# Row-alternated attention products in the second layer, and division after the value products in the third

## Chip, cores and metric

The kernel runs on one core of one Trainium2 chip. The metric is device time in microseconds (us) of one execution, as a median over runs. TensorE is called PE here, its weight loads PEld, VectorE DVE, ScalarE ACT, GpSimd POOL, and SyncE, which issues most transfers, SP.

## The reference

One forward pass over 256 tokens of width 1024 through three layers. The first (latent attention, an RWKV recurrence and 32 experts) is untouched by the change. The second has two attention mixers, the third has one with three branches; both end in a gated feed-forward network. Cut to what the change touches:

```python
# second layer, mixer A ("dsa"): index scores choose keys, then latent attention
rel = relu(einsum('bqhd,bsd->bqhs', iq, ik) * IDX_DIM ** -0.5)       # 8 heads of 64
score = einsum('bqhs,bqh->bqs', rel, iw)                            # causal, top_k(score, 64)
q_lat = einsum('bthd,hdc->bthc', q_nope, w_uk)                      # 8 heads, 64 -> 128
s = einsum('bqhc,bqkc->bqhk', concat[q_lat, q_rope], kg) * A_SCALE  # 128 + 32 deep
o = softmax(s) @ c_kv                                               # then w_uv
# second layer, mixer B ("diff"): two softmaxes m = 0, 1 per head, 4 heads
s = einsum('bqhmd,bshmd->bhmqs', q, k) * B_QK_DIM ** -0.5           # 64 deep
a = softmax(s)[:, :, 0] - lam_full * softmax(s)[:, :, 1]
o = einsum('bhqs,bshe->bqhe', a, v)
# third layer ("nsa"): 16 heads in 4 groups; compressed, selected and window branches
out = g[..., 0:1] * o_cmp + g[..., 1:2] * o_slc + g[..., 2:3] * o_win
```

## The kernel before, in words

Everything lies with tokens or features on the 128 partitions, in two token halves j = 0, 1; half 1 sees 256 keys (nk = 256), half 0 sees 128. Large weights stream from HBM and are split by ACT (`whi`, L304) and DVE or POOL (`wlo`, L308, L306) into two fp32r parts, so that a product is three cheap matmuls (L297 to L299). These run all the time and are called **fill** here: whenever a mixer waits for another engine, PE does fill. Up to six split weight tiles are kept ready ahead of PE.

The mixers' own products are plain fp32. One such product is two records in the trace, since PE makes two passes over each weight load pair. Many of them are only 64 or 32 deep, so that they use rows 0 to 63 or 64 to 127 of PE (or a strip of 32), and leave the other rows free. PSUM has 8 banks; `bank(K)` takes one, of 512 fp32 columns per partition.

**Second layer.** Four generators are interleaved by `weave`: the fill stream, `dsa_index`, `diff` and `dsa`. A generator yields a cost and a lag in us, by which `weave` decides who writes its instructions next; a scheduler then fixes each engine's order, within which every engine works strictly in turn. `pipe` runs a list of units through stages, one unit later per stage.

- `dsa_index`: for each half (1 first) four visits to PE. A visit takes one parity `par` of heads, thus one row half, and does two matmuls (L2063) into one bank; then ReLU on ACT and weighted sums on DVE, later eight rounds of maximum and replacement on DVE.
- `diff`: six units (half, first head, heads, m). Products of a unit (L2235, rows chosen by m) each followed by the causal mask, added by a bf16 matmul with an identity (L2237). Then DVE maximum (L2239), ACT exponentials with sums, division (L2262 combines m = 0 and 1), transposes on PE (L2271), products with the values (L2287).
- `dsa` starts when fill and `diff` are through: `qlT` by eight matmuls of 64 rows (L2105), copied by ACT and DVE (L2110). Then eight units (j, h0) of two heads; per head a 128-deep latent product (L2130), a 32-deep rope product in strip h0 (L2131) and the mask (L2132), all into one bank. Then maximum (L2134), exponentials (L2139), reciprocal and multiply (L2148), and transposes on PE (L2158).

**Third layer.** Here the order is as written. `pace` puts fill between the steps of `nsa`, which sends 28 units through scores, weigh, turn, values and out. 24 are ordinary (one or two heads, two branches s) and 4 are compressed (one per group). `weigh` takes the reciprocal, multiplies by the gate, and scales the 512 columns of exponentials on DVE (L2622); `turn` transposes (L2633), copies; `values` (L2657, L2645) accumulates all units of a group in one long-lived bank, which ACT copies when a half is complete (L2561); `out` transposes.

Of the kernel before, what the change touches and what calls it, by code (L numbers as in the profile page):

```python
# [2011 lines left out]
def dsa_index(K, pool, T, S, D, done):  # L2012
# [42 lines left out]
    for j in (1, 0):  # L2055
# [36 lines left out]
def dsa(K, pool, T, S, D, mix, done):  # L2092
# [8 lines left out]
    for b in range(0, 4, 2):  # L2101
        for par in range(2):
            p = bank(K)
            for bb in range(2):
                nc.tensor.matmul(p[:, bb * 256:bb * 256 + 256], wuk[rows[par], b + bb, :], T["qnT"][rows[par], b + bb, :],  # L2105
                                 start=True, stop=True)
# [6 lines left out]
            yield 0.9  # L2113
# [5 lines left out]
    prs = {}  # L2119

    def scores(u):
        j, h0 = u
        nk = 128 * (j + 1)
        js = slice(j * 128, j * 128 + 128)
        r = slice(h0 * 32, h0 * 32 + 32)
        p = bank(K)
        for i in range(2):
            h = h0 + 4 * i
            o = p[:, i * nk:i * nk + nk]
            nc.tensor.matmul(o, qlT[h % 2][:, h // 2, js], ckvT[:, :nk], start=i == 0, stop=False, skip_group_check=True)  # L2130
            nc.tensor.matmul(o, T["qrT"][r, i, js], krT[r, :nk], start=False, stop=False, skip_group_check=True)  # L2131
            nc.tensor.matmul(o, K.identb, mk[j], start=False, stop=True, skip_group_check=True)  # L2132
# [8 lines left out]
        return 0.98 * (j + 1)  # L2141
# [62 lines left out]
def diff(K, pool, T, S, mix, done):  # L2204
# [21 lines left out]
    prs, aTs, pos = {}, {}, {}  # L2226

    def scores(u):
        j, h0, hp, m = u
        nk = 128 * (j + 1)  # L2230
        js = slice(j * 128, j * 128 + 128)
        p = bank(K)
        for i in range(hp):
            oo = p[:, i * nk:(i + 1) * nk]
            nc.tensor.matmul(oo, qb[rows[m], h0 + i, js], kb[rows[m], h0 + i, :nk], start=i == 0, stop=False,  # L2235
                             skip_group_check=True)
            nc.tensor.matmul(oo[:, js], K.identb, K.causb, start=False, stop=True, skip_group_check=True)  # L2237
# [9 lines left out]
        return 1.1  # L2247
# [265 lines left out]
def nsa(K, pool, T, mix, done):  # L2513
# [34 lines left out]
    pos, mixed = {}, []  # L2548

    def into(u):  # L2550

        new = u.b not in pos
        if new:
            pos[u.b] = bank(K)
        return pos[u.b], new

    def ends(u):
        u.O = {}
        for j in u.ends:
            u.O[j] = pool.tile([128, 256], F32, name="Onsa", bufs=2)  # L2560
            nc.scalar.activation(u.O[j], pos[u.b][:, j * 256:j * 256 + 256], AF.Copy)  # L2561

    def scores(u):
        b = u.b
        if u.j is None:

            pc = bank(K)
            u.pr = s3 = pool.tile([128, 2, 2, 2, 16], F32, name="s3", bufs=2)
# [36 lines left out]
    def weigh(u):  # L2605
# [12 lines left out]
        for ii in range(u.hp):  # L2618
            h = 4 * u.b + 2 * (u.i0 + ii) + u.par
            for s in range(2):  # L2620
                q = (ii * 2 + s) * u.nk
                nc.vector.tensor_scalar(u.pr[:, q:q + u.nk], u.pr[:, q:q + u.nk], den[:, u.j, h, s:s + 1], None, op0=OP.mult)  # L2622

    def turn(u):
        pt = bank(K)
        if u.j is None:
            for j in range(2):
                nc.tensor.transpose(pt[LOP, j * 128:j * 128 + 128], u.pr[:, j].rearrange("p i s n -> p (i s n)"), K.ident)
            u.pT = pool.tile([64, 256], F32, name="pcT", bufs=2)
# [11 lines left out]
    def values(u):  # L2641
        if u.j is None:
            po, new = into(u)
            for j in range(2):
                nc.tensor.matmul(po[:, j * 256:j * 256 + 256], u.pT[:, j * 128:j * 128 + 128],  # L2645
                                 T["vbd"][:, u.b].rearrange("p h d -> p (h d)"), start=new and j == 0, stop=bool(u.ends),
                                 skip_group_check=True)
            ends(u)
            return 0.9
        j, g = u.j, u.b  # L2650
        po, new = into(u)
        for ii in range(u.hp):
            o = j * 256 + (2 * (u.i0 + ii) + u.par) * 64
            for s in range(2):
                for b in range(j + 1):
                    bb = (ii * 2 + s) * (j + 1) + b
                    nc.tensor.matmul(po[:, o:o + 64], u.pT[:, bb * 128:bb * 128 + 128], vsw[:, b, s, g * 64:g * 64 + 64],  # L2657
                                     start=new and ii + s + b == 0, stop=s == 1 and b == j, skip_group_check=True)
        ends(u)
        return 0.9  # L2660

    def out(u):
        for j in u.ends:
            p = bank(K)
            for k in range(2):
                nc.tensor.transpose(p[:, k * 128:k * 128 + 128], u.O[j][:, k * 128:k * 128 + 128], K.ident)
# [228 lines left out]
```

## Time and profile before

| what | value |
|---|---|
| median of 3 runs (lowest, highest) | 1305.43 us (1299.16, 1306.05) |
| the profiled execution, own time | 1300.7 us |
| its span, first to last instruction | 1298.9 us |
| PE busy | 1236.4 us, 95% |
| DVE busy | 905.1 us, 70% |
| ACT busy | 746.3 us, 57% |
| POOL busy | 161.8 us, 12% |
| mean granted PE clock | 0.979 of full speed |

Times inside the span count from its start. The second layer's mixers stand at about 570 to 712 us, the third's at about 960 to 1090 us. A matmul's start is a record; its end is modelled and overlaps the next one's start, so prices here go from start to start. The granted clock has two levels, 1.0 (2.4 GHz) and 0.5 (1.2 GHz); a mean between them tells the share of each.

### The profile page before, as it was taken

What the parts mean: (1) busy time and instruction counts of PE and PEld (TensorE: products, weight loads), DVE (VectorE), ACT (ScalarE), POOL (GpSimd) and SP (SyncE); (2) the same over time, 40 slices, a digit from 0 to 9 for tenths busy, and PEclk for the clock granted to TensorE, in tenths of its full rate; (3) what the DMA queues carried; (4) which work ended last, traced back from release to release, by engine and by line L of the source; (5) the groups of instructions that cost most, each with busy time, mean ns of one, the idle gap of its engine ahead of it and who ended that gap; (6) DMA issues with size and microseconds to landing.
All of it is one profiled execution on the core that took longest, in us unless ns stands there. A gap on an engine that the chain in (4) does not pass through costs nothing.

```text
span 1298.9 us, 21081 instructions
## 1 busy us (share of the span) xinstructions
PE 1236.4 (95%) x7798; PEld 1072.3 (83%) x7798; DVE 905.1 (70%) x1779; ACT 746.3 (57%) x1540; POOL 161.8 (12%) x245
## 2 busy tenths in 40 slices
PE   7898999999989999999999999999899998999997
PEld 7687998778868888788866899988878877999986
DVE  5688546889989999867966555564567776655462
ACT  6864314779879898764453444454355554544451
POOL 7134002000010000011110000000057321000000
PEclk9899989889989999999999999999999999999999
DMA  9322007788979999564312365575242313655560
GB/s 282 112 98 82 1 2 241 256 291 334 344 268 336 338 382 321 167 189 143 113 50 65 114 196 172 186 249 173 89 129 85 111 33 98 202 173 172 184 227 33
DMA packets 124282, 228.71 MB, mean 176 GB/s; under 512 B 10720, under 2 KB 86832, under 8 KB 124176
## 3 DMA queue, kind: packets, MB, share of 16 engines
q1 hardware_dynamic: 122672, 223.83, 50.5%
q0 software_dynamic: 1504, 3.49, 1.0%
q8 instruction: 63, 1.03, 0.3%
q14 instruction: 43, 0.35, 0.1%
HBM read 226.25 MB, written 1.05 MB: 175 GB/s over the span
## 4 chain that ended last, share of the span: by engine, by line
PE 48%; DVE 4%; ACT 2%; issue 1%; DMA 1%; POOL 0%; DVEq 0%; POOLq 0%; ACTq 0%
PE ps L297 13%; PE ps L299 13%; PE ps L298 13%; PE ps L2657 1%; DMA raw<-in_ev_w_in_dram 1%; DVE pr L2622 1%; DVE wlo L308 1%; PE ps L1918 1%; PE ps L2633 1%; PE ps L2235 1%; PE ps L2131 1%; PE ps L2592 1%; PE ps L2475 1%; PE ps L2063 1%; ACT whi L304 0%
## 5 line engine op out<-in xcount | busy, mean ns | idle before, releaser
L308 DVE TENSOR_TENSOR wlo<-raw,whi 128x512 fp32r<-128x512 f32 (+1 forms) x797 | 510.9, 690 | 79.4 <-ACT whi L304 77.2
L304 ACT ACTIVATE whi<-raw 128x512 fp32r<-128x512 f32 (+1 forms) x821 | 476.9, 625 | 123.1 <-PE ps L299 38.3
L297 PE MATMUL ps<-hTh,whi 128*128 128x256 f32 (+1 forms) x1032 | 301.3, 292 | 1.2 <-ACT whi L304 1.2
L299 PE MATMUL ps<-hTh,wlo 128*128 128x256 f32 (+1 forms) x1032 | 292.2, 283 | 0.2 <-DVE wlo L308 0.2
L298 PE MATMUL ps<-hTl,whi 128*128 128x256 f32 (+1 forms) x1032 | 291.8, 283 | 0.0
L297 PEld LDWEIGHTS ps<-hTh,whi 128*128 128x128 f32 (+1 forms) x1032 | 196.5, 190 | 6.0 <-issue 3.2
L298 PEld LDWEIGHTS ps<-hTl,whi 128*128 128x128 f32 (+1 forms) x1032 | 197.3, 191 | 2.7 <-issue 2.4
L299 PEld LDWEIGHTS ps<-hTh,wlo 128*128 128x128 f32 (+1 forms) x1032 | 196.0, 190 | 0.4 <-DVE wlo L308 0.4
L297 PE MATMUL ps<-whi,xh 128*128 128x512 f32 x256 | 104.2, 407 | 0.0
L298 PE MATMUL ps<-wlo,xh 128*128 128x512 f32 x256 | 101.8, 397 | 0.0
L299 PE MATMUL ps<-whi,xl 128*128 128x512 f32 x256 | 101.5, 397 | 0.0
L272 POOL TENSOR_TENSOR nrs<-nv,mhalf 128x1 f32<-128x1 f32 x10 | 5.6, 556 | 629.6 <-DVE nv L1716 629.6
L304 ACT ACTIVATE hh<-sl 128x512 fp32r<-128x512 f32 x20 | 12.6, 632 | 115.0 <-DVE sl L1808 115.0
L1808 DVE TENSOR_TENSOR sl<-sl,ps 128x512 f32<-128x512 f32 x20 | 13.8, 688 | 88.8 <-PE ps L299 88.8
L298 PE MATMUL ps<-wlo,hh 128*128 128x512 f32 x176 | 69.6, 395 | 0.0
L297 PE MATMUL ps<-whi,hh 128*128 128x512 f32 x176 | 69.3, 394 | 0.0
L297 PE MATMUL ps<-whi,hTh 128*128 128x256 f32 (+3 forms) x192 | 61.0, 319 | 6.3 <-ACT hTh L304 4.4
L299 PE MATMUL ps<-whi,hTl 128*128 128x256 f32 (+3 forms) x192 | 60.4, 316 | 1.3 <-DVE hTl L308 1.3
L298 PE MATMUL ps<-wlo,hTh 128*128 128x256 f32 (+3 forms) x192 | 60.0, 313 | 0.8 <-DVE wlo L308 0.8
L299 PEld LDWEIGHTS ps<-whi,xl 128*128 128x128 f32 x256 | 48.5, 189 | 11.1
L297 PEld LDWEIGHTS ps<-whi,xh 128*128 128x128 f32 x256 | 48.6, 190 | 10.1
L298 PEld LDWEIGHTS ps<-wlo,xh 128*128 128x128 f32 x256 | 48.7, 190 | 9.9
(878 smaller groups left out, 2218.5 us busy)
## 6 DMA issues: line engine op xcount, KB each, us to landing
raw<-in_w_gate_dram SPq DMA_DIRECT2D x64, 512.0 KB, 5.2
raw<-in_w_up_dram SPq DMA_DIRECT2D x64, 512.0 KB, 6.1
raw<-in_w_down_dram SPq DMA_DIRECT2D x32, 1024.0 KB, 6.8
raw<-in_ffn_w_gate_dram SPq DMA_DIRECT2D x22, 1024.0 KB, 5.4
raw<-in_ffn_w_up_dram SPq DMA_DIRECT2D x22, 1024.0 KB, 5.9
raw<-in_ffn_w_down_dram SPq DMA_DIRECT2D x22, 1024.0 KB, 5.1
raw<-in_ev_w_in_dram SPq DMA_DIRECT2D x11, 1024.0 KB, 5.7
raw<-in_od_w_in_dram SPq DMA_DIRECT2D x10, 1024.0 KB, 5.2
```

What stands on the lines that cost most here:

```text
L297: nc.tensor.matmul(ps, lh, rh, start=start, stop=False, **kw)
L298: nc.tensor.matmul(ps, lh, rl, start=False, stop=False, **kw)
L299: nc.tensor.matmul(ps, ll, rh, start=False, stop=stop, **kw)
L304: K.nc.scalar.activation(hi, src, AF.Copy)
L308: K.nc.vector.tensor_tensor(lo, src, hi.bitcast(F32), op=OP.subtract)
L1808: nc.vector.tensor_tensor(sl, sl, pu, op=OP.mult)
L1918: nc.tensor.matmul(p2, c[f"R{d}"], z.rearrange("p b t -> p (b t)"), start=True, stop=True)
L2063: nc.tensor.matmul(p[:, bb * nk:bb * nk + nk], T["iqT"][rows[par], b0 + bb, j * 128:j * 128 + 128], ikT[rows[par], :nk], start=True, stop= ...
L2131: nc.tensor.matmul(o, T["qrT"][r, i, js], krT[r, :nk], start=False, stop=False, skip_group_check=True)
L2235: nc.tensor.matmul(oo, qb[rows[m], h0 + i, js], kb[rows[m], h0 + i, :nk], start=i == 0, stop=False, skip_group_check=True)
L2475: nc.tensor.matmul(p[:, :60], w1[:, i, :], tmp[:, i].rearrange("p g n -> p (g n)"), start=i == 0, stop=i == 15)
L2592: nc.tensor.matmul(o, q2[r], KL[r, b, :, :u.nk], start=False, stop=False, skip_group_check=True)
```

## The change

In the second layer, products that use different rows of PE are issued alternately into two banks: index visits take both parities at once, `diff` takes m = 0 and 1 in one visit, `dsa` takes the units h0 and h0 + 1 in one visit, with rope products of two strips alternating and masks last. The yielded costs follow. In the third layer, exponentials are transposed undivided; each unit's values go to a bank of its own, and DVE divides, gates and adds the 64 columns of each head and branch from PSUM into an SBUF sum. The compressed units' scores and their transposes move to the common ring of 8 tiles (`w2k`).

```diff
             for par in range(2):
-                p = bank(K)
-                for bb in range(2):
-                    nc.tensor.matmul(p[:, bb * nk:bb * nk + nk], T["iqT"][rows[par], b0 + bb, j * 128:j * 128 + 128],
-                                     ikT[rows[par], :nk], start=True, stop=True)
+            ps = [bank(K), bank(K)]
+            for bb in range(2):
+                for par in range(2):
+                    nc.tensor.matmul(ps[par][:, bb * nk:bb * nk + nk], T["iqT"][rows[par], b0 + bb, j * 128:j * 128 + 128],
+                                     ikT[rows[par], :nk], start=True, stop=True)
...
-                yield 0.43 * (j + 1), 0.8
+                yield 0.25 * (j + 1), 0.8
...
+    def products(j, hs):
+        nk = 128 * (j + 1)
+        js = slice(j * 128, j * 128 + 128)
+        for h0 in hs:
+            sps[j, h0] = bank(K)
+        o = lambda h0, i: sps[j, h0][:, i * nk:i * nk + nk]
+        for h0 in hs:
+            for i in range(2):
+                h = h0 + 4 * i
+                nc.tensor.matmul(o(h0, i), qlT[h % 2][:, h // 2, js], ckvT[:, :nk], start=i == 0, stop=False, skip_group_check=True)
+        for i in range(2):
+            for h0 in hs:
+                r = slice(h0 * 32, h0 * 32 + 32)
+                nc.tensor.matmul(o(h0, i), T["qrT"][r, i, js], krT[r, :nk], start=False, stop=False, skip_group_check=True)
+        for h0 in hs:
+            for i in range(2):
+                nc.tensor.matmul(o(h0, i), K.identb, mk[j], start=False, stop=True, skip_group_check=True)
...
-        return 0.98 * (j + 1)
+        return 1.5 * (j + 1) if h0 % 2 == 0 else 0.0
...
+    def products(j, h0, hp):
+        nk = 128 * (j + 1)
+        js = slice(j * 128, j * 128 + 128)
+        ps = [bank(K), bank(K)]
+        for i in range(hp):
+            for m in range(2):
+                nc.tensor.matmul(ps[m][:, i * nk:(i + 1) * nk], qb[rows[m], h0 + i, js], kb[rows[m], h0 + i, :nk], start=i == 0,
+                                 stop=False, skip_group_check=True)
+        for m in range(2):
+            for i in range(hp):
+                nc.tensor.matmul(ps[m][:, i * nk:(i + 1) * nk][:, js], K.identb, K.causb, start=False, stop=True,
+                                 skip_group_check=True)
+            sps[j, h0, hp, m] = ps[m]
...
-        for ii in range(u.hp):
-            h = 4 * u.b + 2 * (u.i0 + ii) + u.par
-            for s in range(2):
-                q = (ii * 2 + s) * u.nk
-                nc.vector.tensor_scalar(u.pr[:, q:q + u.nk], u.pr[:, q:q + u.nk], den[:, u.j, h, s:s + 1], None, op0=OP.mult)
...
+        for ii in range(u.hp):
+            i = 2 * (u.i0 + ii) + u.par
+            oh = O[:, i * 64:i * 64 + 64]
+            for s in range(2):
+                o = po[:, (ii * 2 + s) * 64:(ii * 2 + s) * 64 + 64]
+                d = den[:, j, 4 * g + i, s:s + 1]
+                if (g, j, i) in begun:
+                    nc.vector.scalar_tensor_tensor(oh, o, d, oh, op0=OP.mult, op1=OP.add)
+                else:
+                    nc.vector.tensor_scalar(oh, o, d, None, op0=OP.mult)
+                begun.add((g, j, i))
```

The order of the instructions at three places. First PE at the start of `dsa`, where `qlT` is made (buffer numbers shown; ps_7731, ps_7735 and so on are banks). Before:

```order
L1918 MATMUL ps_7724<-rz_7721,cst_b_6659 128x512
L2105 MATMUL ps_7731<-qnT_7438,wuk2_2343 128x256 x2
L2105 MATMUL ps_7735<-qnT_7438,wuk2_2343 128x256 x2
L2105 MATMUL ps_7739<-qnT_7438,wuk2_2343 128x256 x2
L2105 MATMUL ps_7743<-qnT_7438,wuk2_2343 128x256 x2
L2130 MATMUL ps_7751<-ckvT_6892,qlT0_7729 128x256
```

Now:

```order
L1918 MATMUL ps_7724<-rz_7721,cst_b_6659 128x512
L2108 MATMUL ps_7731<-qnT_7443,wuk2_2343 128x256
L2108 MATMUL ps_7732<-qnT_7443,wuk2_2343 128x256
L2108 MATMUL ps_7731<-qnT_7443,wuk2_2343 128x256
L2108 MATMUL ps_7732<-qnT_7443,wuk2_2343 128x256
L2108 MATMUL ps_7739<-qnT_7443,wuk2_2343 128x256
L2108 MATMUL ps_7740<-qnT_7443,wuk2_2343 128x256
L2108 MATMUL ps_7739<-qnT_7443,wuk2_2343 128x256
L2108 MATMUL ps_7740<-qnT_7443,wuk2_2343 128x256
```

The eight matmuls are the same and back to back in both; two of one row half in a row became one of each in turn.

Second, PE a little later, up to the first transposes of `dsa` (pr2_7760 and pr2_7767 are the first unit's exponentials). Before, the second unit and six transposes of `diff`'s output stand ahead of them:

```order
L2130 MATMUL ps_7767<-ckvT_6892,qlT1_7730 128x256
L2131 MATMUL ps_7767<-krT_6893,qrT_7720 128x256
L2132 LDWEIGHTS identb_370
L2132 MATMUL ps_7767<-selm_7311,identb_370 128x256
L2308 MATMUL ps_7779<-cst_i_90,odf_7423 128x128 x2
L2308 MATMUL ps_7784<-cst_i_90,odf_7423 128x128 x2
L2308 MATMUL ps_7789<-cst_i_90,odf_7423 128x128 x2
L2158 MATMUL ps_7795<-cst_i_90,pr2_7760 128x128 x4
```

Now:

```order
L2141 MATMUL ps_7751<-krT_6893,qrT_7720 128x256
L2141 MATMUL ps_7752<-krT_6893,qrT_7720 128x256
L2141 MATMUL ps_7751<-krT_6893,qrT_7720 128x256
L2141 MATMUL ps_7752<-krT_6893,qrT_7720 128x256
L2144 LDWEIGHTS identb_370
L2144 MATMUL ps_7751<-selm_7311,identb_370 128x256
L2144 LDWEIGHTS identb_370
L2144 MATMUL ps_7751<-selm_7311,identb_370 128x256
L2144 LDWEIGHTS identb_370
L2144 MATMUL ps_7752<-selm_7311,identb_370 128x256
L2144 LDWEIGHTS identb_370
L2144 MATMUL ps_7752<-selm_7311,identb_370 128x256
L2177 MATMUL ps_7780<-cst_i_90,pr2_7767 128x128 x4
```

The products of units 0 and 1 come together, and the transposes of unit 0 follow the last mask with nothing between; the transposes of `diff`'s output (L2308, now L2338) come only after units 2 and 3.

Third, DVE in one step of the third layer, as one piece of the difference (`Onsa` is the new sum):

```order
-L2616 RECIPROCAL den_10402<-den_10402 128x2
-L2617 TENSOR_TENSOR den_10402<-den_10402,gts 128x2
-L2622 TENSOR_SCALAR pr_10882<-pr_10882,den_10402 128x256 x2
-L2638 COPY pT_10960<-ps 128x512
-L2595 TENSOR_REDUCE mx_10401<-ps 128x2x2
+L2639 RECIPROCAL den_10402<-den_10402 128x2
+L2640 TENSOR_TENSOR den_10402<-den_10402,gts 128x2
+L2656 COPY pT_10955<-ps 128x512
+L2618 TENSOR_REDUCE mx_10401<-ps 128x2x2
+L2697 TENSOR_SCALAR Onsa<-ps,den_10402 128x64
+L2695 SCALAR_TENSOR_TENSOR Onsa<-ps,den_10402,Onsa 128x64
 L1921 TENSOR_TENSOR qf<-ps,qf 128x512
```

The two multiplies of 256 columns ahead of the copy and the maximum are gone; two operations of 64 columns from PSUM stand behind them. On PE the order of the third layer's products is what it was.

## Rows read from the trace of the kernel before

**Rows 1.** Windows: us, busy time and instructions of PE, PEld, DVE, ACT, POOL, clock, DMA, GB/s.
```profile
560.00:600.00 40.00, 37.70 (x290) 36.36 (x289) 26.04 (x47) 21.81 (x45) 6.70 (x18) 0.94 0.64 198
600.00:640.00 40.00, 40.00 (x265) 33.42 (x264) 34.50 (x87) 15.99 (x30) 0.00 (x0) 1.00 0.39 132
...
1050.00:1080.00 30.00, 25.97 (x139) 19.31 (x139) 23.95 (x53) 14.56 (x49) 12.49 (x12) 0.94 0.16 52
1080.00:1100.00 20.00, 20.00 (x101) 16.72 (x100) 13.21 (x27) 8.40 (x20) 0.57 (x1) 0.91 0.42 135
```
**Rows 2.** Waits of PE from 940 to 1110 us: total, times, longest.
```profile
PE ps L2633 <- DVE pr L2622: 7.7, 10, 1.5
```
**Rows 3.** Timeline of PE in the first layer: start, busy, line, operands, count.
```profile
114.49 1.16 PE L960 MATMUL ps<-bt,AR 64*128 64x128 f32 x16
...
127.26 1.13 PE L990 MATMUL ps<-AR,kt 64*128 64x256 f32 x8
```
**Rows 4.** Timeline of PE, index visits of half 1 and of half 0.
```profile
602.88 0.28 PE L298 MATMUL ps<-hTl,whi 128*128 128x256 f32 x1
603.00 0.28 PE L299 MATMUL ps<-hTh,wlo 128*128 128x256 f32 x1
603.21 1.13 PE L2063 MATMUL ps<-ikT,iqT 64*128 64x256 f32 x4
...
604.50 0.28 PE L298 MATMUL ps<-hTl,whi 128*128 128x256 f32 x1
...
626.58 0.71 PE L2063 MATMUL ps<-ikT,iqT 64*128 64x128 f32 x4
```
**Rows 5.** Timeline of PE in `diff`, a unit of half 1 and one of half 0.
```profile
636.49 0.70 PE L2235 MATMUL ps<-kbT,qbT 64*128 64x256 f32 x2
...
638.15 0.28 PE L298 MATMUL ps<-hTl,whi 128*128 128x256 f32 x1
...
654.30 0.48 PE L2235 MATMUL ps<-kbT,qbT 64*128 64x128 f32 x2
...
656.68 0.28 PE L298 MATMUL ps<-hTl,whi 128*128 128x256 f32 x1
```
**Rows 6.** Timeline of PE in `dsa`: `qlT`, a head of half 1, a head of half 0.
```profile
665.82 2.10 PE L2105 MATMUL ps<-qnT,wuk 64*128 64x256 f32 x16
...
669.22 0.60 PE L2130 MATMUL ps<-ckvT,qlT 128*128 128x256 f32 x2
669.75 0.69 PE L2131 MATMUL ps<-krT,qrT 32*128 32x256 f32 x2
...
670.50 0.60 PE L2130 MATMUL ps<-ckvT,qlT 128*128 128x256 f32 x2
...
685.53 0.39 PE L2130 MATMUL ps<-ckvT,qlT 128*128 128x128 f32 x2
...
686.33 0.44 PE L2130 MATMUL ps<-ckvT,qlT 128*128 128x128 f32 x2
```
**Rows 7.** Timeline of DVE at the start of `dsa`.
```profile
669.17 1.28 DVE L2110 COPY qlT<-ps 128x512 f32<-128x512 f32 x2
670.70 0.69 DVE L2134 TENSOR_REDUCE mx<-ps 128x2 f32<-128x512 f32 x1 [0.24 <-PE ps L2132]
...
673.85 0.68 DVE L2148 TENSOR_TENSOR pr<-pr,den 128x512 f32<-128x512 f32 x1
```
**Rows 8.** Timeline of PE, first transposes of `dsa`.
```profile
674.68 0.63 PE L2158 MATMUL ps<-cst_i,pr 128*128 128x128 f32 x4 [0.82 <-ACT mxh L2309]
```
**Rows 9.** Groups by line from 940 to 1110 us: busy, mean ns, idle before.
```profile
L2622 DVE TENSOR_SCALAR pr<-pr,den 128x256 f32<-128x256 f32 (+1 forms) x64 | 30.8, 536 | 1.2
```
**Rows 10.** Line L2622 on DVE: shortest, median and longest in ns.
```profile
L2622 DVE TENSOR_SCALAR pr<-pr,den x64: 272/349/1370, 970.1 to 1081.2; 128x256 f32<-128x256 f32 x32, 128x128 f32<-128x128 f32 x32
```
**Rows 11.** Timeline of DVE: a small copy from PSUM; one late unit's multiplies.
```profile
962.99 0.25 DVE L2366 COPY gts<-ps 128x96 f32<-128x96 f32 x1
...
1075.81 3.92 DVE L2622 TENSOR_SCALAR pr<-pr,den 128x128 f32<-128x128 f32 x4
```

More of the change, by code (lines that the diff above doesn't have):

```diff
@@ L2101, in dsa @@
     for b in range(0, 4, 2):
+        ps = [bank(K), bank(K)]
+        for bb in range(2):
+            for par in range(2):
+                nc.tensor.matmul(ps[par][:, bb * 256:bb * 256 + 256], wuk[rows[par], b + bb, :], T["qnT"][rows[par], b + bb, :],
+                                 start=True, stop=True)
         for par in range(2):
[L2103 to L2106, printed above, removed]
+            p = ps[par]
             dst = qlT[par][:, b:b + 2, :]
@@ L2123, in scores @@
         nk = 128 * (j + 1)
[L2124 to L2132, printed above, removed]
+        if h0 % 2 == 0:
+            products(j, (h0, h0 + 1))
+        p = sps.pop(u)
         mv = mx[:, j, h0:8:4]
@@ L2230, in scores @@
         nk = 128 * (j + 1)
[L2231 to L2237, printed above, removed]
+        if m == 0:
+            products(j, h0, hp)
+        p = sps.pop(u)
         mv = mx[:, j, m, h0:h0 + hp]
@@ L2246, in scores @@
                                  accum_out=den[:, j, m, h:h + 1])
-        return 1.1
+        return 0.0 if m else 1.4
     def weigh(u):
@@ L2547, in nsa, with into @@
             [u for u in g if u.j == 1][-1].ends = (1,)
[L2548 to L2561, printed above, removed]
+    sums, begun, mixed = {}, set(), []
+    def into(b, j):
+        if (b, j) not in sums:
+            sums[b, j] = pool.tile([128, 256], F32, name="Onsa", bufs=5)
+        return sums[b, j]
     def scores(u):
@@ L2641, in values @@
     def values(u):
+        po = bank(K)
         if u.j is None:
-            po, new = into(u)
             for j in range(2):
                 nc.tensor.matmul(po[:, j * 256:j * 256 + 256], u.pT[:, j * 128:j * 128 + 128],
-                                 T["vbd"][:, u.b].rearrange("p h d -> p (h d)"), start=new and j == 0, stop=bool(u.ends),
-                                 skip_group_check=True)
-            ends(u)
+                                 T["vbd"][:, u.b].rearrange("p h d -> p (h d)"), start=True, stop=True)
+            for j in range(2):
+                O = into(u.b, j)
+                old = [i for i in range(4) if (u.b, j, i) in begun]
+                begun.update((u.b, j, i) for i in range(4))
+                cuts = [(i, i + 1) for i in range(4)] if 0 < len(old) < 4 else [(0, 4)]
+                for i, n in cuts:
+                    o, oh = po[:, j * 256 + i * 64:j * 256 + n * 64], O[:, i * 64:n * 64]
+                    if i in old:
+                        nc.vector.tensor_tensor(oh, o, oh, op=OP.add)
+                    else:
+                        nc.vector.tensor_copy(oh, o)
@@ L2649, in values @@
             return 0.9
         j, g = u.j, u.b
-        po, new = into(u)
+        O = into(g, j)
         for ii in range(u.hp):
-            o = j * 256 + (2 * (u.i0 + ii) + u.par) * 64
             for s in range(2):
+                o = po[:, (ii * 2 + s) * 64:(ii * 2 + s) * 64 + 64]
                 for b in range(j + 1):
                     bb = (ii * 2 + s) * (j + 1) + b
-                    nc.tensor.matmul(po[:, o:o + 64], u.pT[:, bb * 128:bb * 128 + 128], vsw[:, b, s, g * 64:g * 64 + 64],
-                                     start=new and ii + s + b == 0, stop=s == 1 and b == j, skip_group_check=True)
@@ L2659, in values @@
-        ends(u)
+                    nc.tensor.matmul(o, u.pT[:, bb * 128:bb * 128 + 128], vsw[:, b, s, g * 64:g * 64 + 64],
+                                     start=b == 0, stop=b == j)
+        for ii in range(u.hp):
+            i = 2 * (u.i0 + ii) + u.par
+            oh = O[:, i * 64:i * 64 + 64]
+            for s in range(2):
+                o = po[:, (ii * 2 + s) * 64:(ii * 2 + s) * 64 + 64]
+                d = den[:, j, 4 * g + i, s:s + 1]
+                if (g, j, i) in begun:
+                    nc.vector.scalar_tensor_tensor(oh, o, d, oh, op0=OP.mult, op1=OP.add)
+                else:
+                    nc.vector.tensor_scalar(oh, o, d, None, op0=OP.mult)
+                begun.add((g, j, i))
```

14 lines of the change are left out of this document (8 added, 6 removed).

## The prediction

> **What bounds the kernel now.** I read the windows first. In the second layer PE is the limit: from 600 to 640 us it is busy 40.00 of 40 us, while DVE has 34.50 [rows 1]. So matmul time saved there should show, as long as DVE, which has little left, keeps up. In the third layer PE is not full: 25.97 of 30 us from 1050 to 1080 [rows 1]. The waits say for what: the transposes (L2633) wait for the multiply of the exponentials on DVE (L2622), 7.7 us in ten waits [rows 2]. The clock column adds a second cost: it reads 0.94 from 1050 to 1080 and 0.91 from 1080 to 1100 us, where it is 1.00 at full speed [rows 1], that is, stretches at 1.2 instead of 2.4 GHz that begin among these waits.
>
> What a row-alternated product costs need not be guessed, since the first layer does it already. L990 alternates row halves and puts 8 records of 256 columns into 1.13 us [rows 3]; L2063, on one row half, needs 1.13 us for 4 [rows 4]. At 128 columns, L960 puts 16 records into 1.16 us [rows 3], against 0.71 us for 4 [rows 4]. Two row halves run at the same time, and a visit with twice the products costs what a visit costs now.
>
> **Index.** A fill step is 0.12 us (602.88 to 603.00). From the last fill matmul before a visit to the second one after it are 1.50 us; less two steps, a visit of half 1 costs 1.26 us [rows 4]. This includes about 0.1 us at each end, the switch between 128 and 64 rows (0.21 us from 603.00 to 603.21 instead of 0.12). A visit of half 0 is 1.13 - 0.71 = 0.42 us shorter: 0.84. Four visits per half become two: 2 x 1.26 + 2 x 0.84 = **4.2 us** saved.
>
> **qlT.** The order of the eight matmuls changes from two and two to alternating. I count nothing: the 16 records take 2.10 us now, 0.13 us each [rows 6], where L2063's take 0.28 [rows 4]. They overlap already, though they are not issued alternately; both halves must only be in PE's queue. The Trainium skill, "TensorE: Matmul & The Clock Gate", Part 3, says that matmuls start strictly in program order. By that rule a pair's second half could start only at the last record of its first, 13 steps of 0.22 us instead of 8, about 2.9 us, and the alternation would save 0.8 us; the row's 2.10 us speaks against it.
>
> **diff.** A unit of half 1 lasts 1.66 us from its first matmul to the second fill matmul, with the lead-in and less a step 1.63; four units are 6.5 us [rows 5]. Now there are two visits of 1.26 us with four masks behind. A mask of 128 bf16 columns is between half a fill step and a whole one, 0.06 to 0.12; I take 0.08, nearer to half, since it has half the columns. That makes 2 x 1.6 = 3.2, so 3.3 saved. Of half 0, a unit is 2.38 us in the same terms, 2.3 net, two are 4.6 [rows 5]; now once 1.16 + 0.1 for the sixteen records and 8 x 0.08 for masks, 1.9; 2.7 saved. Together **6.0 us**.
>
> Part of it comes back. The transposes of a unit wait for DVE's maximum and combination, and DVE shares this stretch with the index's eight rounds and the splits. PE gets some 6 us earlier to the first transposes (4.2 and one visit pair's 1.7). DVE's free time in 600 to 640 is 5.5 us [rows 1], and part of it is forced by dependencies. Bounds are 0 and 6.0; I take **2.4 us** back, as if 3.6 of the 5.5 can be used. The split tiles are no risk at this size: six are ready ahead.
>
> **dsa.** A head of half 1 takes 1.28 us: 0.53 for the latent product with its switch, 0.75 for rope and mask [rows 6]. The mask is a fill step, the rope 0.63, with its switch 0.73. The four ropes of two units, 2.9 us, become one visit of 1.2 (L990's 1.13 and a lead-in): 1.7 saved, 3.4 for two pairs. A head of half 0 takes 0.80 [rows 6]; the rope is half of the 0.42 cheaper, 0.52, four are 2.1 and become 0.8: 1.3, for two pairs 2.6. Together **6.0 us**.
>
> Here the order takes something away. Before, the second unit and six other transposes stand between the first unit's products and its transposes, and PE still idles 0.82 us [rows 8]. Now nothing stands between, and fill has run out. The chain is maximum, exponentials, reciprocal, multiply: from 670.70 to 674.53, 3.83 us [rows 7]. It begins before the last mask; PE then stands still between 3.2 (one maximum less) and 3.8 us; I take 3.4, which is **2.6 us** more than now. Also, the third latent product needs `qlT` of odd heads, copied at 669.17 and ready about 669.8 [rows 7]; PE, which ends `qlT` at 667.9 [rows 6] and then does two latent products in 1.0, would be there at 668.9: **0.9 us** lost. And the clock may fall. From 560 to 600 us PE idles 2.3 us and the mean clock is 0.94, 2.4 us lost; 0.06 of 30 us, 1.8 us, are lost in 1050 to 1080 [rows 1]. I count **1.8 us** for the new idle stretch; the bounds are 0 and 2.4.
>
> **Third layer.** PE's products and their order stay. L2622 goes, 30.8 us of DVE [rows 9]. A small copy from PSUM, 96 columns, takes 0.25 us [rows 11]; 64 new operations of 64 columns take at most that, 16 us, and eight of 256 columns for the compressed units, at 0.4 (below the 0.68 of 512 columns [rows 7]), 3.2. DVE gets 12 us lighter, and what is left of it stands behind the maximum. The multiplies were also erratic: median 349 ns, longest 1370 [rows 10], four of 128 columns in 3.92 us [rows 11]. The transposes will wait for the exponentials alone, done before the multiplies begin. I let 1.0 of the 7.7 us stay, for the first units, which PE reaches soonest: **6.7 us** saved, bounds 0 and 7.7. If the waits go, so should the two slow stretches: 1.8 + 0.09 x 20 = **3.6 us**, bounds 0 and 3.6.
>
> **The sum.** 4.2 + 6.0 + 6.0 - 2.4 - 2.6 - 0.9 - 1.8 + 6.7 + 3.6 = 18.8 us. Against the profiled execution's own 1300.7 us that is 1281.9. This execution lies 4.7 us below the median of 1305.43; on the median it would be 1286.6. I forecast 1284, between.
>
> **Rivals.**
> - *DVE and ACT take over in the second layer.* For: DVE's 34.50 of 40 us [rows 1]. Against: after 640 us the index is nearly through. Then the rest of what `diff` and `dsa` gain is lost too, 3.6 + 0.7 = 4.3 us, and each of the two further idle stretches costs up to 1.8 of clock: 1284 + 4.3 + 1.8 = 1290. The Trainium skill, "TensorEngine Tiling (Array Packing)", section PSUM Bottleneck, warns of just this, that tiling speeds up PE but not the emptying of PSUM.
> - *Everything is covered.* No clock loss at the start of `dsa` (1.8), nothing back in `diff` (2.4), no wait left in the third layer (1.0): 1284 - 5.2 = 1279. For: six split tiles and fill between the steps of `diff`.
> - *The third layer's wait moves.* The transposes then wait for ACT or for banks, and one clock stretch stays; 3 of the 10.3 us remain as gain: 1291. Against: the late multiplies alone take 3.92 us [rows 11].
> - *No overlap in the new order.* If the products ran one after another, 16.2 us would not come, nor the 2.4 be given back: 1284 + 13.8 = 1298. Against it stand rows 3 and L2105.
> - *Slower.* One place: DVE in the third layer. The new operations wait for PE's value products, and the next step's maximum, copies and reciprocals queue behind them. If DVE were then the limit of each step, all 19 us of them would stand on the path, and the 10.3 us of gain be lost: 1284 + 19 + 10.3 = 1313. It decides from the point where DVE is full in 960 to 1080 us; now it has 23.95 of 30 [rows 1], and gets lighter.
>
> **How the numbers follow.** Forecast 0.48, DVE and ACT 0.18, all covered 0.17, moved wait 0.10, no overlap 0.04, slower 0.03. The range of 1274 to 1294 holds the first four with 4 to 5 us around them, about the spread of the runs. A measurement of this kernel can tell about 0.5% (6.5 us) from no change. Below 1298.9: 0.92. Within: 0.05, mostly no overlap. Slower: 0.03.
>
> **What would show it.** Right: index visits in half the number, with 8 records in 1.1 us; `qlT` still about 2.1 us; PE idle some 3.4 us before the first transposes of `dsa`, and a clock below 1.0 soon after; in the third layer, waits of L2633's successor on DVE gone, the clock 1.00 from 1050 to 1100. Wrong: waits of PE on DVE of several us from 640 to 665 us, DVE full in the third layer, or records of the two row halves that start 0.2 us apart.

## The result, and the profile after

The changed kernel takes 1280.53 us (median of 4, 1278.99 to 1280.94) beside 1303.26 for the kernel before: ratio 0.9833, interval 0.9807 to 0.986. The forecast was 1284, the range 1274 to 1294. The profiled execution's span is 1278.3 us, against 1298.9.

Where the 20.6 us come from is read best from the starts of the same matmuls in both traces. Ahead of the first index visit the new execution is 0.6 us early, which is no work of the change. At the first product of `diff` it is 4.8 us early (631.72 against 636.49 [rows 5]), at `qlT` 8.0 (657.84 against 665.82 [rows 6]), at the first transposes behind the second layer's mixers still 8.0 (713.0 against 721.0), at the start of the third layer's attention 8.0 (950.8 against 958.8), and behind it 20.8 (1078.2 against 1099.0). So index gave 4.2, `diff` 3.2, `dsa` nothing, and the third layer 12.8. The starts compare equal work: ahead of the first product of `diff`, for one, both traces have 2112 records of fill and 1394 others.

The windows of the changed kernel (columns as in [rows 1]):

```profile
600.00:640.00 40.00, 38.98 (x303) 34.31 (x302) 37.61 (x105) 18.42 (x37) 1.84 (x2) 1.00 0.39 132
640.00:665.00 25.00, 21.41 (x158) 16.82 (x158) 17.75 (x46) 12.75 (x39) 5.85 (x7) 1.00 0.27 85
665.00:690.00 25.00, 21.42 (x109) 15.46 (x110) 16.04 (x39) 11.20 (x36) 0.00 (x0) 0.86 0.09 24
1050.00:1080.00 30.00, 29.27 (x162) 23.59 (x160) 23.31 (x57) 14.98 (x46) 5.98 (x6) 1.00 0.34 106
1080.00:1100.00 20.00, 18.89 (x153) 18.25 (x154) 12.02 (x21) 10.91 (x21) 1.18 (x2) 1.00 0.42 132
```

From 600 to 640 us PE now does 303 matmuls where it did 265 [rows 1], and DVE is at 37.61 of 40 us. In the third layer the clock is 1.00 and PE nearly full. The price stands in the row 665 to 690: 3.6 us of idle PE and a clock of 0.86, thus 0.14 x 25 = 3.5 us lost. The waits of PE from 595 to 712 us say for what:

```profile
PE ps L2177 <- DVE pr L2167: 3.4, 1, 3.4
PE ps L2317 <- ACT aT L2303: 1.6, 2, 0.9
PE ps L2301 <- DVE pr L2292: 1.0, 1, 1.0
PE ps L2137 <- DVE qlT L2115: 0.9, 1, 0.9
PE ps L1918 <- DVE rz L1910: 0.9, 1, 0.9
PE ps L2193 <- DVE den L2166: 0.2, 1, 0.2
```

And those from 947 to 1075 us, the whole third layer's attention, where 7.7 us stood [rows 2] and the transposes (now L2651) no longer occur:

```profile
PE ps L1918 <- DVE rz L1913: 0.5, 2, 0.3
PE ps L2614 <- POOL q L2364: 0.3, 1, 0.3
PE ps L2646 <- POOL s L2636: 0.2, 1, 0.2
```

The timeline of PE shows a merged index visit and the first products of `diff`:

```profile
602.41 0.28 PE L299 MATMUL ps<-hTh,wlo 128*128 128x256 f32 x1
602.62 1.13 PE L2064 MATMUL ps<-ikT,iqT 64*128 64x256 f32 x8
...
603.90 0.28 PE L298 MATMUL ps<-hTl,whi 128*128 128x256 f32 x1
...
631.72 1.14 PE L2254 MATMUL ps<-kbT,qbT 64*128 64x256 f32 x8
632.78 0.40 PE L2258 MATMUL ps<-causb,identb 128*128 128x128 bf16 x4
```

From the last fill matmul before the visit to the second one after it are 1.49 us, for eight records; before it was 1.50 for four [rows 4]. The start of `dsa`, in the same view:

```profile
657.84 2.00 PE L2108 MATMUL ps<-qnT,wuk 64*128 64x256 f32 x16
659.77 1.45 PE L2137 MATMUL ps<-ckvT,qlT 128*128 128x256 f32 x4
662.15 1.30 PE L2137 MATMUL ps<-ckvT,qlT 128*128 128x256 f32 x4 [0.93 <-DVE qlT L2115]
663.38 1.13 PE L2141 MATMUL ps<-krT,qrT 32*128 32x256 f32 x8
...
668.42 1.09 PE L2177 MATMUL ps<-cst_i,pr 128*128 128x128 f32 x4 [3.37 <-DVE pr L2167]
669.30 3.62 PE L2137 MATMUL ps<-ckvT,qlT 128*128 128x256 f32 x8
672.85 1.52 PE L2141 MATMUL ps<-krT,qrT 32*128 32x256 f32 x8
```

Eight latent records (L2137), which take 1.99 us in a run below where the clock is 1.00, take 3.62 behind the idle stretch: that is the clock at 1.2 GHz. The new work of DVE in the third layer, from 950 to 1100 us (groups by line):

```profile
L2695 DVE SCALAR_TENSOR_TENSOR Onsa<-ps,den,Onsa 128x64 f32<-128x64 f32 x37 | 10.3, 283 | 1.7 <-PE ps L2686 0.6
...
L2697 DVE TENSOR_SCALAR Onsa<-ps,den 128x64 f32<-128x64 f32 x27 | 7.5, 278 | 1.4 <-PE ps L2686 0.2
...
L2673 DVE TENSOR_TENSOR Onsa<-ps,Onsa 128x256 f32<-128x256 f32 (+1 forms) x9 | 2.7, 345 | 0.2 <-PE ps L2663 0.2
```

20.5 us, and 21.1 with two copies of the same sums (L2675, 0.6), beside 30.8 that went [rows 9].

### The profile page after: what moved, and what is told of

The parts are those of the page before. It is cut to its first block, busy times and chain, and to the rows that moved or that the text cites. A ratio compares the mean times of both kernels' runs of the same rounds, so it can differ in the third digit from the quotient of the medians.

```text
span 1278.3 us, 21070 instructions
## 1 busy us (share of the span) xinstructions
PE 1216.7 (95%) x7798; PEld 1063.3 (83%) x7798; DVE 891.3 (70%) x1790; ACT 743.0 (58%) x1532; POOL 161.3 (13%) x245
## 4 chain that ended last, share of the span: by engine, by line
PE 46%; DVE 5%; ACT 2%; issue 1%; POOL 1%; DMA 1%; DVEq 0%; POOLq 0%; ACTq 0%
PE ps L299 13%; PE ps L297 13%; PE ps L298 13%; PE ps L2686 1%; DVE wlo L308 1%; PE ps L2615 1%; PE ps L2651 1%; ACT whi L304 1%; PE ps L2505 1%; DMA raw<-in_ev_w_in_dram 1%; PE ps L1918 1%; PE ps L2137 1%; DVE acc L2084 0%; PE ps L2193 0%; PE ps L2616 0%
## 5 line engine op out<-in xcount | busy, mean ns | idle before, releaser
L297 PE MATMUL ps<-hTh,whi 128*128 128x256 f32 (+1 forms) x1032 | 301.2, 292 | 1.2 <-ACT whi L304 1.2
L297 PEld LDWEIGHTS ps<-hTh,whi 128*128 128x128 f32 (+1 forms) x1032 | 196.5, 190 | 5.5 <-issue 2.7
L297 PE MATMUL ps<-whi,xh 128*128 128x512 f32 x256 | 104.2, 407 | 0.0
L297 PE MATMUL ps<-whi,hh 128*128 128x512 f32 x176 | 69.3, 394 | 0.0
L297 PE MATMUL ps<-whi,hTh 128*128 128x256 f32 (+3 forms) x192 | 61.1, 319 | 6.3 <-ACT hTh L304 4.4
L297 PEld LDWEIGHTS ps<-whi,xh 128*128 128x128 f32 x256 | 48.8, 191 | 10.1
```

What stands on the lines that cost most here:

```text
L297: nc.tensor.matmul(ps, lh, rh, start=start, stop=False, **kw)
```

## The experiments

**One layer at a time.** First the second layer's change alone, then the third's alone.

```diff
 # second only: nsa as before
-                    nc.vector.tensor_scalar(oh, o, d, None, op0=OP.mult)
+                nc.vector.tensor_scalar(u.pr[:, q:q + u.nk], u.pr[:, q:q + u.nk], den[:, u.j, h, s:s + 1], None, op0=OP.mult)
...
 # third only: dsa_index, dsa and diff as before
-            products(j, (h0, h0 + 1))
...
```

> The change to the second layer (index, diff, dsa) alone; the third layer is as before. The working of the prediction gives 4.2 + 6.0 + 6.0 - 2.4 - 2.6 - 0.9 - 1.8 = 8.5 us saved, about 1294.8 us beside 1303.3, ratio 0.9935. The starts of the same matmuls in the two traces say 7.4 us (shift -0.6 at 592 us, -8.0 at 721 us): ratio 0.9943. Rival, the parts interact (what the second layer gains comes only with the lighter third layer, or the reverse): then this run and the third layer's run do not add up to 22.7 us, by 3 us or more.

> The change to the third layer (division and gate after the value products) alone; the second layer is as before. The working of the prediction gives 6.7 + 3.6 = 10.3 us saved, about 1293, ratio 0.992. The starts of the same matmuls say 12.8 us (shift -8.0 at 958 us, -20.8 at 1099 us): 1290.5, ratio 0.990. If the waits and the two slow stretches go for the reason given, PE waits at most 1 us in all for DVE in the third layer's transposes here too, and the granted clock is 1.00 from 1050 to 1100 us. Rival, the slow stretches went because the second layer's change shifted the third layer against its transfers: then the clock still falls here and the run stays above 1293.

Measured: 1292.03 us, ratio 0.9926 (0.9908 to 0.9944), and 1286.01, 0.9901 (0.9871 to 0.9931), beside 1300.42. The savings of 8.4 and 14.4 us add up to 22.8; the whole change gave 22.7. No interaction shows, though the three intervals together leave room for some 5 us. With the second layer alone, the transposes' waits are there as before (one line of the waits from 945 to 1100 us, and windows). The clock falls there too, and for longer than in the profile of the kernel before: it reads 0.89 from 950 to 980 us, which was 1.00, and 0.84 from 1050 to 1080, which was 0.94. This profile is of the slowest of the six executions (1297.0 us; the others 1289.0 to 1294.1).

```profile
PE ps L2663 <- DVE pr L2652: 7.1, 8, 1.5
```

```profile
950.00:980.00 30.00, 27.46 (x166) 22.03 (x165) 20.88 (x38) 15.89 (x48) 16.57 (x14) 0.89 0.36 105
1050.00:1080.00 30.00, 25.97 (x124) 19.61 (x124) 22.60 (x49) 11.11 (x40) 10.65 (x10) 0.84 0.22 71
```

With the third layer alone, no such wait is left and the clock is full, so in this execution it was not the shift of the third layer that cleared it:

```profile
1050.00:1080.00 30.00, 30.00 (x170) 24.27 (x169) 24.54 (x63) 15.05 (x45) 7.25 (x9) 1.00 0.39 126
1080.00:1100.00 20.00, 18.16 (x137) 16.68 (x136) 12.63 (x22) 10.23 (x20) 1.63 (x3) 1.00 0.46 145
```

From the same first to the same last matmul, the third layer's attention takes 127.4 us here and in the changed kernel, 140.2 before: 12.8 us again. This is one execution. The six of the run lie from 1282.6 to 1296.4 us at mean clocks from 0.987 down to 0.975, so others lost clock somewhere, in a place that no trace shows.

**Alternation, or only the same visit?**

```diff
-            for bb in range(2):
-                for par in range(2):
+            for par in range(2):
+                for bb in range(2):
                     nc.tensor.matmul(ps[par][:, bb * nk:bb * nk + nk], ...
```

and likewise in `diff` (m outside) and for the ropes of `dsa` (h0 outside).

> The changed kernel, but within each visit the products of one row half are all issued before those of the other (index, diff, and dsa's rope products by quarter); visits, banks and what is issued between them stay. If both halves only have to be in PE's queue, the records still start in pairs some 10 to 20 ns apart, 8 of 256 columns take 1.13 us as in the changed kernel, and the time is 1280.5 within 1.5. If a matmul cannot start before all earlier ones have started, the second half begins at the last record of the first: 3 x 0.28 = 0.84 us more per visit at 256 columns and 3 x 0.14 = 0.42 at 128; index 2.5, diff 1.7 + 1.0, ropes 0.8, together some 6 us: 1286.5, ratio 0.987 to 0.988.

Measured: 1282.58, 0.9858 (0.984 to 0.9876). The timeline of PE:

```profile
602.36 0.28 PE L299 MATMUL ps<-hTh,wlo 128*128 128x256 f32 x1
602.57 1.14 PE L2064 MATMUL ps<-ikT,iqT 64*128 64x256 f32 x8
...
603.87 0.28 PE L298 MATMUL ps<-hTl,whi 128*128 128x256 f32 x1
...
631.70 1.14 PE L2254 MATMUL ps<-kbT,qbT 64*128 64x256 f32 x8
```

The visit takes 1.51 us in the same terms. The records still start in pairs, 14 ns apart (7 ns when alternated), although the second half's first product stands behind the first half's second one in the program. All through index the run keeps step with the changed kernel within 0.1 us. It loses 2.4 us later, none of it in a visit: 0.7 up to `qlT`, where `diff`'s transposes waited 1.6 instead of 1.0 us for DVE, and 1.7 in `dsa`, where the slow stretch behind the 3.4 us wait lasted longer (0.80 from 665 to 690 us instead of 0.86). So in these visits the alternation is worth nothing; it is enough that both halves are in PE's queue without a wait between them. All four runs (1281.5 to 1284.0) lie above all nine of the changed kernel in this study (1276.2 to 1280.9); so with this order something behind the visits costs 2 to 3 us, and how that comes about is open.

**The idle stretch of `dsa`.** Products one pair of units ahead:

```diff
-        if h0 % 2 == 0:
-            products(j, (h0, h0 + 1))
+        c = {(1, 0): (1, 0), (1, 1): (1, 2), (1, 3): (0, 0), (0, 1): (0, 2)}.get(u)
+        if c: products(c[0], (c[1], c[1] + 1))
```

> The changed kernel, with the scores' products of dsa issued one pair of units ahead (the second pair's products stand before the first transposes, which waited 3.4 us for DVE). Theory: the idle stretch of 3.4 us goes, since 3 us of products and 0.9 of output transposes now stand in it, and the stretch of 6.8 us at 1.2 GHz behind it, which costs 3.4 us, goes with it: 1280.5 - 6.8 = 1273.7, ratio 0.977 to 0.978. Rival one, the fall of the clock has another cause: 1277, a slow stretch near 667 us stays. Rival two, the wait only moves to the next transposes or to a bank: 1280 or more.

Measured: 1281.18, 0.9841 (0.9815 to 0.9868), and this median hides two groups, three runs from 1276.6 to 1278.1 and three from 1284.3 to 1286.5. The profile is of the second group. The mean clock tells the groups apart: 0.980 to 0.982 in the quicker one, 0.972 to 0.976 in the other. In `dsa` the run does gain 4.5 us, as matmul starts show, with no slow stretch near 667 us. The theory said 6.8; later waits took up some of it, such as 1.5 us for DVE's copy of the turned weights (L2193), where 0.2 stood. It loses 11.7 us in the third layer, whose instructions are those of the changed kernel. Windows of the run with the products ahead, then of its L297 alone (fill's first matmul; busy and counts of PE and PEld, clock, DMA, GB/s):

```profile
1018.00:1041.00 23.00, 23.00 (x85) 17.45 (x85) 12.62 (x42) 7.78 (x32) 2.01 (x5) 0.50 0.00 0
```

```profile
1018.00:1041.00 23.00, 0.00 (x0) 0.00 (x0) 0.50 0.00 0
```

PE is full and at half clock. There is no fill in this stretch, in any of the kernels: in the changed kernel it lasts from 1010.3 to 1037.9 us, at full clock. Here it begins at 1004.0, the clock falls at 1018.2 and comes back at 1045.5, 3.9 us after fill returns at 1041.6.

Then with the ropes, which need no `qlT`, ahead of the latent products as well:

```diff
+        for i in range(2):
+            for h0 in hs:
+                r = slice(h0 * 32, h0 * 32 + 32)
+                nc.tensor.matmul(o(h0, i), T["qrT"][r, i, js], krT[r, :nk], start=i == 0, ...
         for h0 in hs:
             for i in range(2):
                 h = h0 + 4 * i
-                nc.tensor.matmul(o(h0, i), qlT[h % 2][:, h // 2, js], ckvT[:, :nk], start=i == 0, ...
+                nc.tensor.matmul(o(h0, i), qlT[h % 2][:, h // 2, js], ckvT[:, :nk], start=False, ...
```

> As the run with the products one pair ahead, and the rope products stand before the latent products, so that the copies of qlT are covered too. In the second layer the wait of 3.4 us for the multiply and the one of 0.9 for qlT go, and no slow stretch near 667 us: 1280.5 - 4.5 (the shift measured within dsa with the products ahead) - 0.9 - 0.2 = 1275, ratio 0.978 to 0.979, in executions without a long slow stretch in the third layer. If the stretch of 27 us in the third layer of the earlier run was brought on by the earlier start, it shows here too and the time is 1284 to 1286 in part of the runs; if it was chance of that execution, it may be absent.

Measured: 1274.05, 0.9782 (0.9763 to 0.9801), all five runs from 1271.3 to 1275.3: the best kernel of the study. Its timeline and one window:

```profile
660.54 1.13 PE L2137 MATMUL ps<-krT,qrT 32*128 32x256 f32 x8
...
662.92 1.30 PE L2141 MATMUL ps<-ckvT,qlT 128*128 128x256 f32 x4 [0.19 <-DVE qlT L2115]
...
665.64 1.99 PE L2141 MATMUL ps<-ckvT,qlT 128*128 128x256 f32 x8
...
668.57 0.60 PE L2177 MATMUL ps<-cst_i,pr 128*128 128x128 f32 x4
```

```profile
665.00:690.00 25.00, 24.41 (x154) 18.40 (x151) 20.12 (x51) 13.45 (x46) 0.00 (x0) 1.00 0.14 43
```

The first transposes wait for nothing, 0.19 us of 0.93 is left at `qlT`, and the clock stays at 1.00: eight latent records take 1.99 us. In `dsa` matmul starts gain 5.4 us.

And the other way round, `dsa` in the old order:

```diff
-            products(j, (h0, h0 + 1))
+            nc.tensor.matmul(o, qlT[h % 2][:, h // 2, js], ckvT[:, :nk], start=i == 0, stop=False, skip_group_check=True)
...
```

> The changed kernel with dsa's products in the old order (unit by unit, qlT two and two). The working of the prediction makes dsa's part worth 6.0 - 2.6 - 0.9 - 1.8 = 0.7 us, so 1281.2. The traces say 0.1 (shift -7.9 at 658 us, -8.0 at 713 us), so 1280.6: everything that the quicker products save is given back in the idle stretch ahead of the first transposes and by the clock behind it. Here the wait of 3.4 us should be about 0.8 as before, and no slow stretch stands near 667 us. If it comes out over 1284, the order in dsa is worth more than the traces show.

Measured: 1279.4, 0.983 (0.9812 to 0.9848): no slower than the changed kernel. The wait ahead of the first transposes and the clock are those of the kernel before:

```profile
PE ps L2161 <- ACT mxh L2323: 0.8, 1, 0.8
```

```profile
665.00:690.00 25.00, 24.18 (x116) 16.27 (x114) 16.78 (x39) 10.57 (x34) 0.00 (x0) 1.00 0.14 43
```

Yet its matmul starts are 0.76 us ahead of the changed kernel's at `qlT` and 0.76 ahead behind `dsa`. As built, `dsa`'s part is worth nothing.

**The third layer: the place in the chain, or DVE's load?** Three kernels put DVE work back where the multiplies stood. In the first the transposes wait for it; in the others nobody reads the result.

```diff
 # chain kept
+        for q in range(0, 512, u.nk):
+            nc.vector.tensor_scalar(u.pr[:, q:q + u.nk], u.pr[:, q:q + u.nk], 1.0, None, op0=OP.mult)
 # load kept (range(2)), load half (range(1))
+        for s in range(2):
+            nc.vector.tensor_reduce(spare[:, s:s + 1], u.pr, axis=AX.X, op=OP.max)
```

> The changed kernel with DVE multiplies of the exponentials by 1.0 put back where the old multiplies stood (same count, same widths, in place, so that the transposes wait for them); division and gate after the value products stay, so DVE has some 30 us more work in the third layer. If the third layer's gain came from taking the multiply out of the chain maximum, exponentials, multiply, transposes: the transposes wait for DVE some 7 to 8 us in ten places again, and about 1.6 us more are lost since an idle PE starts anew (a record lasts 0.28 us, a step 0.12), and one or two slow stretches of the clock may return: 1290 to 1293, ratio 0.990 to 0.993. If the gain came from elsewhere (sums in separate banks, less copying on ACT): it stays near 1281.

> The changed kernel with two maxima over 512 columns per unit added on DVE where the old multiplies stood, into a spare tile that nobody reads: 48 operations of about 0.65 us, 31 us of DVE work, as much as the old multiplies took, but nobody waits for their result. If it was the place in the chain: PE's transposes still do not wait for DVE by more than 1.5 us in all, and the time is 1280.5 to 1283, ratio 0.984 to 0.986. If it was DVE's load: the waits return at the maxima and copies that queue behind, 1288 or more, ratio 0.989 or more. This is also the rival of the prediction on the slower side, DVE as the limit, made stronger.

> The changed kernel with one spare maximum over 512 columns per unit (24 operations of 0.68 us, 16 us of DVE work, instead of the 30.5 us of the run with two): DVE's load in the third layer is then about that of the kernel before (which has 30.8 us of multiplies against 20.5 us of new operations and sums). If the place in the chain decides, PE's waits for DVE there stay under 2 us in all and the time is 1280 to 1283 where no long slow stretch begins near 1020 us; such a stretch would cost 13.7 us (27.3 us at half speed), the clock column tells it. If DVE's load decides, some 7 us of waits return as in the kernel before: 1288 or more without any long slow stretch.

Measured: chain kept 1300.37, 0.9987 (0.9972 to 1.0001); load kept 1304.56, 1.0024 (1.001 to 1.0037); half the load 1297.95, 0.9967 (0.995 to 0.9984). All three lie near the kernel before. The theory of the place had 1290 to 1293 for the first and 1280 to 1283 for the others, there without a long slow stretch of the clock, and all three have one. The load kept is what its rival said. The waits from 945 to 1100 us, of the chain kept:

```profile
PE ps L2653 <- DVE pr L2642: 4.1, 5, 1.2
...
PE ps L2653 <- ACT pT L2656: 0.6, 1, 0.6
```

of the load kept:

```profile
PE ps L2689 <- DVE pT L2659: 3.6, 3, 1.7
PE ps L2649 <- POOL s L2637: 0.9, 1, 0.9
```

of half the load:

```profile
PE ps L2689 <- DVE pT L2659: 1.3, 2, 1.1
...
PE ps L2649 <- POOL s L2637: 0.9, 1, 0.9
```

With 16.2 us put back off the chain, 6 more than the kernel before has in all, PE waits 2.2 us there, not 7.7; so the place counts. With 30.5 us off the chain it waits 4.5, now for copies that queue behind on DVE; so the load counts too. The chain kept waits 4.7, and not 7.7, though the transposes again wait for the multiplies. But the waits are the small part. Half the load, two windows:

```profile
1025.00:1052.00 27.00, 27.00 (x107) 21.45 (x106) 18.16 (x62) 9.82 (x39) 2.42 (x6) 0.51 0.00 0
1055.00:1075.00 20.00, 19.08 (x103) 15.29 (x103) 15.65 (x42) 9.22 (x35) 6.76 (x8) 0.87 0.17 53
```

In the stretch without fill the clock is at half for 27 us, which costs 13; the other two show the same, from 1028.2 for 27.3 us and from 1020.5 for 41.0. All end within 4.2 us of fill's return. From 1010 to 1100 us half the load loses 17 us by the clock (0.76, 0.78 and 0.89 in three windows of 30 us). The next table takes the clock out. It goes from the same first to the same last matmul of the third layer's attention and counts half the length of each slow stretch in it as lost, which holds if PE is the limit there, as the full PE of the windows says:

| kernel | attention, us | lost by the clock | the rest, above the changed kernel |
|---|---|---|---|
| changed | 127.4 | 0 | 0 |
| before | 140.2 | 3.4 | 9.4 |
| chain kept | 147.2 | 15.4 | 4.3 |
| load kept | 151.8 | 20.5 | 3.9 |
| half the load | 145.6 | 17.1 | 1.0 |

Without the clock, half the load costs 1.0 us, as the place says; at 30.5 us off the chain the load costs as much as the chain kept. The chain kept gives back 4.3 of the 9.4 us. Its multiplies are quicker than those of before (394 ns in the mean, not 536 [rows 9]), and it keeps what else the change brought to the third layer: a bank for each unit's values, the ring of 8 tiles, and eight copies less on ACT (L2561, 2.7 us before). No run takes these apart, so some 5 of the 9.4 us are not pinned to the place.

**Last, the changed kernel again, and `diff`'s values one step later.**

```diff
-..., (0, 0, 4, 1)], [scores, weigh, turn, values], 1.0)
+..., (0, 0, 4, 1)], [scores, weigh, turn, skip, values], 1.0)   # skip = lambda u: 0.0
```

> The changed kernel once more, beside the others. 1280.5, ratio 0.982 to 0.985. Open: whether one of its executions shows the long slow stretch in the third layer that three other kernels showed (that execution would be at 1290 to 1294).

> The changed kernel with diff's value products one step later, so that fill stands between the copy of the turned weights and the products that wait for it. The two waits for ACT's copy, 0.9 and 0.6 us, go, with 0.16 us each for a PE that starts anew: 1280.5 - 1.9 = 1278.6, a step below what the time alone can tell; the trace has to show it between 636 and 658 us. Rival: the wait only moves to the next transposes or to the last group, which lies ahead of dsa without fill: 1280.5 or more.

> The changed kernel with all three: dsa's products one pair ahead, ropes ahead of the latent products, diff's value products one step later. From the run with the first two (ratio 0.9782) less 1.9 us: ratio 0.9768, 1273 beside 1303. If the clock takes the gain back (a slow stretch that the other run did not have), 1276 or more.

Measured: the changed kernel 1279.23, 0.9818 (0.9793 to 0.9843), no run over 1280.4; values later 1281.81, 0.9847 (0.9823 to 0.9871); all three 1278.94, 0.9828 (0.9801 to 0.9855). The rival was right for the second, and the third falls behind the two edits alone (0.9782). Waits of PE from 595 to 715 us with the values later:

```profile
PE ps L2177 <- DVE pr L2167: 3.4, 1, 3.4
PE ps L2301 <- DVE pr L2292: 2.4, 2, 1.3
PE ps L2137 <- DVE qlT L2115: 2.0, 1, 2.0
PE ps L1918 <- DVE rz L1910: 0.8, 1, 0.8
PE ps L2317 <- ACT aT L2303: 0.4, 1, 0.4
```

The wait for ACT shrinks by 1.2 us; the last values now stand behind all fill, and the transposes and `qlT` wait 2.5 us more. The clock falls near 654 us (0.93 of 25 us, 1.8 lost), and loses as much less behind the 3.4 us wait (0.93 from 665 to 690 us instead of 0.86).

## Why the prediction was right, point by point

The forecast was 3.5 us above the measured median. The sum of 18.8 us stands against 4.2 + 3.2 + 0.0 + 12.8 = 20.2 in the traces. Two terms missed, `dsa` by 0.7 and the third layer by 2.5, with opposite signs, so that it is partly luck that the total is nearer than the parts.

- **Index, 4.2.** 4.8 - 0.6 = 4.2 us. A visit costs what it cost, with twice the records. Shown by the trace.
- **diff, 6.0 - 2.4 = 3.6.** 3.2 us. What comes back is 2.8 us, of which the waits show 2.6; only 1.0 is the wait for DVE that the step named, 1.6 are two waits for ACT's copy of the turned weights. DVE uses 37.61 of 40 us from 600 to 640, so 3.1 of the 5.5 us of free time could be used; I had said 3.6.
- **qlT, nothing for the alternation.** 2.00 us against 2.10. The run with the halves one after another shows the same for index and `diff`: records of the two halves start 14 ns apart. The rule of the Trainium skill ("TensorE: Matmul & The Clock Gate", Part 3) that matmuls start strictly in program order does not agree with these rows; by it, that run was expected 6 us slower.
- **dsa, 6.0 - 2.6 - 0.9 - 1.8 = 0.7.** 0.0. The wait is 3.37 (3.4 said), `qlT` 0.93 (0.9 said). The step that failed is the clock, taken at 1.8 with a bound of 2.4: it cost 3.5. The bound came from another stretch, and from a window that holds only part of it: in the kernel before, the clock reads 0.66 from 557 to 562 us and 0.66 from 588 to 593, 1.7 us lost in each, 3.4 and not 2.4. Nor does one stretch bound the next: behind the same wait the load kept lost 1.8 us (0.93 of 25) and the run half by half 5.0 (0.80). The link itself is well shown: all eight traces with the wait of 3.4 us have a slow stretch that begins in it or behind it, the six without it none from 660 to 690 us. With the measured wait and clock the sum would be -0.9 and not 0.0; one later wait of 0.6 us became 0.2, and what else makes up the difference no run splits.
- **Third layer, 6.7 + 3.6 = 10.3.** 12.8 by the traces, 14.4 by the times of the run with it alone (interval 9 to 17). The clock's 3.6 came in full. The waits of PE fell from 7.7 + 0.8 to 1.0. The mis-sized term is the wait: a wait's row counts from the modelled end of the last record, 0.28 us after its start, while without a wait the next one starts after 0.12. By this estimate each wait costs some 0.16 more than its row; ten are 1.6. 7.5 + 1.6 + 3.6 = 12.7. That the multiply's place is all of it is not shown: with the chain kept, 4.3 of the 9.4 us outside the clock came back.
- **DVE's new operations, 16 + 3.2.** 17.8 + 3.3 (2.7 and the two copies). The operations of 64 columns take 0.28 us, not the 0.25 that I gave as their most.
- **DVE and ACT take over**, the rival at 1290, named two further idle stretches at up to 1.8 us each and added 1.8 for both; in full they make 1292. It did not come.
- **The slower rival** was put too far off. I let it decide only once DVE is full in 960 to 1080 us. The run with half the load is back near the time of before with 16.2 us more of DVE. The mechanism is another, too: not DVE as the limit of each step, but waits of about a microsecond and a clock that falls in the stretch without fill. Taking the multiply out of the chain is not all of the gain, then; in these runs it kept its worth only with the lighter DVE.

Open: what decides whether the clock falls in the stretch without fill. In the run with products ahead PE's last wait before it was one of 0.3 us, 11 us earlier; the kernel before had waits there (0.8 us at 1031) and kept 1.00. The three kernels with more DVE work lie from 1294.0 to 1307.8 in all 36 runs. The changed kernel's nine lie from 1276.2 to 1280.9. So added DVE work goes with the fall, but the run with products ahead shows that it is not needed for it. No run here took DVE's load away further, or put fill into that stretch.

## What to carry to other kernels

Products that use different row halves should be in one visit; how they are ordered within it made no difference to the visit itself (and 2 to 3 us behind it here). When PE's part of a short softmax chain gets quicker, ask first what independent products can stand ahead of the first transposes: in `dsa` the quicker products were worth nothing until the next pair was issued ahead, and 5 us after. Look for stretches without wide fill before DVE work is added or left there: in the three kernels that added it, the clock cost 15 to 21 us there and behind, and the rest 1 to 4.

## What was not expected of the hardware

- PE at 100% busy can run at half clock for 27 to 41 us. It did in four kernels, always between two pieces of fill, in a stretch of 28 us at full clock where most matmuls have 32 to 128 columns, and never beyond 5 us after fill came back. In other executions of one of these kernels, with the products ahead, the mean clock was up to 0.982 against 0.974, so the same instructions need not bring it. The Trainium skill ("TensorE: Matmul & The Clock Gate", Part 1) says that activity of PE releases its clock; a full busy column, as here, is no sign of that.
- The second row half's first record starts 14 ns after the first half's, although another product of the first half stands between them in the program.
- The 64 multiplies of the kernel before took 536 ns in the mean [rows 9]; those of the chain kept, of the same shapes but with a constant in place of a column, 394 (21.5 us). Which difference between the kernels makes this, the operand or the work beside them, was not tried.
